# A two-layer encoder trunk whose matmuls walk their columns backwards

## The chip, the cores and the metric

The kernel runs on one NeuronCore of a Trainium2 chip. The metric is the device time of one execution in microseconds (us), lower is better. A profile of one execution was recorded for the kernel before the change; its times are those of the instructions on each engine: TensorE (PE, with its weight loads as PEld), VectorE (DVE), ScalarE (ACT), GpSimd (POOL), and SyncE (SP), which issues the DMAs.

## The reference

Two inputs of 512 tokens by 1024 features, "prompt" and "sample", pass through the same two layers. Layer 0 is differential attention, layer 1 a bidirectional retention; each is preceded by an RMS norm and added to the residual, and a final RMS norm closes the trunk. Cut to what matters:

```python
# layer 0, per token block
proj = h @ w_in                        # 1024 -> 8192: q, k, v, gate
q = rotary_half(q) * DA_HEAD_DIM ** -0.5; k = rotary_half(k)
p = softmax(q @ k.T)                   # two maps per head, 8 heads
a = p[:, :, 0] - lam * p[:, :, 1]
o = rms_norm(a @ v, subln_g) * (1 - lambda_init)
x = x + (o * silu(gate)) @ w_out       # 2048 -> 1024

# layer 1
proj = h @ w_in                        # 1024 -> 6144: q, k, v, gate
scores = (q @ k.T) * decay_mask        # within a chunk; forward and backward in time
o = scores @ v + (q * decay) @ state   # state carries k.T @ v of the other chunks
x = x + (rms_norm(o, subln_g) * silu(gate)) @ w_out

y = rms_norm(x, final_norm_g)
```

## The kernel before

**Precision.** Operands are split in two: `hi`, the value rounded to the type fp32r (a copy on ScalarE, `hi_of`, line 399), and `lo`, the value minus `hi` (a subtraction on VectorE, `lo_of`, line 402). A product is three matmuls, hi by hi, hi by lo and lo by hi, accumulated in one PSUM bank (`PASSES`, line 32). So every product below is a run of matmuls in threes. The transposes (lines 606, 716, 815, 1028, 1040, 1161) and eight warm-up matmuls at the start (line 1010) work on plain fp32.

**Projections.** Both input projections go by one step of Strassen's scheme: seven products P1 to P7 instead of eight, whose inputs are sums and differences of blocks. The combined activations are made once per layer (`make_b`, line 448) and stay on chip as `b` tiles or in the `arena`. Class `Unit` (line 518) handles a strip of weights: `prep` combines and splits a weight block, `product` runs the matmuls, `evac` empties the banks. A "pair" unit holds weights as the stationary operand and moves 512 tokens (line 599); a "wide" unit holds activations and moves 256 weight columns into half a bank (line 609).

**Attention and retention.** `scores` (line 1107) makes a 128 by 512 block of scores per map (line 1116); maximum (`row_max`, line 1124), exponential (line 1134), combination and transpose follow (line 1161), then `av` (line 1170) multiplies by the values in 24 matmuls of 256 columns (line 1181). For the retention, `score2` (line 1315), `state2` (line 1339) and `av2` (lines 1359 and 1367) do the like in chunks of 256 tokens.

**Output projection.** `out_step` (line 871) runs six matmuls of 512 columns into a bank (line 891), and VectorE adds the bank, scaled, to the residual. The very last one is done in two halves of 256 columns.

**Order.** All operations are recorded in a `Plan` (line 69) with an assumed cost and with what they read and write. `Plan.arrange` lists them by those costs and by their due times, and the instructions are then issued in that order on each engine's queue. PSUM has four kinds of banks: `pj` (3), `sc` (2), `o` (2) and `tp` (1). The costs handed to the plan are constants in the code (for instance 2.79 us for a pair product of twelve matmuls, line 620), so the order doesn't depend on how a matmul addresses its columns.

A matmul call names the bank, the stationary operand, the moving operand, and whether it opens and closes the accumulation. The one at line 599:

```python
nc.tensor.matmul(
    ps.t, a[u][0]()[:, k, :], bt[k][:, v, :], start=(opens and k == 0 and i == 0),
    stop=(k == 3 and i == 2), skip_group_check=True)
```

The first argument is the output (a bank `ps`, 128 partitions by 512 fp32 columns), the second the stationary operand (128 by 128), the third the moving operand, 128 by 512.

Of the kernel before, what the change touches and what calls it, by code (L numbers as in the profile page):

```python
# [15 lines left out]
P = 128  # L16
# [237 lines left out]
def trunk_kernel(  # L254
# [7 lines left out]
    nc = tc.nc  # L262
# [255 lines left out]
    class Unit:  # L518
# [67 lines left out]
        def product(self, op):  # L586
            which = BANK_OF[op]
            n_banks = 2 if self.wide else 1
            opens = op in OPENS
            if opens:  # L590
                self.banks[which] = [bank(self.tags[which], which) for _ in range(n_banks)]
            a, b = self.ops.pop(op), B_OF[op]
            bt = [Bop[b, k] for k in range(4)]
            reads = [q[1] for q in a] + bt

            def pair(ps, ks=range(4)):
                for k in ks:
                    for i, (u, v) in enumerate(PASSES):
                        nc.tensor.matmul(  # L599
                            ps.t, a[u][0]()[:, k, :], bt[k][:, v, :], start=(opens and k == 0 and i == 0),  # L600
                            stop=(k == 3 and i == 2), skip_group_check=True)

            def wide(ps, t):
                if self.led and op == "P1" and t == 0:
                    for j in range(NT):
                        nc.tensor.transpose(ps[:, j * P:(j + 1) * P], ident.t, ident.t)
                for k in range(4):
                    for i, (u, v) in enumerate(PASSES):
                        nc.tensor.matmul(  # L609
                            ps[:, (t % 2) * 256:(t % 2) * 256 + 256], bt[k][:, v, t * P:(t + 1) * P],  # L610
                            a[u][0]()[:, k, :], start=(opens and t % 2 == 0 and k == 0 and i == 0),
                            stop=(k == 3 and i == 2), skip_group_check=True)

            if not self.wide:
                ps = self.banks[which][0]
                if op == "P1" and self in first_units[:2]:
                    for k in range(4):
                        pe(0.7, lambda k=k: pair(ps, (k,)), reads[:2] + [bt[k]], [(ps, k)])
                else:
                    pe(2.79, lambda: pair(ps), reads, [ps])  # L620
                return
            for t in range(NT):
                ps = self.banks[which][t // 2]
                led = self.led and op == "P1" and t == 0
                pe(1.87 if led else 1.43, lambda ps=ps, t=t: wide(ps, t), reads + [ident] * led, [ps])
# [245 lines left out]
    def out_step(w, h, g, t, i, o, rr, last, parts=1):  # L871


        owed[h, g] -= 1
        if (h, i) not in wsn:
            out_weights(w, h, i)
        banks = [bank("pj") for _ in range(parts)]
        u = wsn[h, i]
        x = xN[g, t]
        n = S // parts  # L880
        for p in range(parts):
            here = slice(p * n, (p + 1) * n)
            part = (x, i) if parts == 1 else (x, (i, p))

            ps = banks[p]

            def fn(here=here, ps=ps):
                m = 0
                for e in range(2):
                    for a, b in PASSES:  # L890
                        nc.tensor.matmul(ps[:, here], o[a][:, e, t * P:(t + 1) * P], u[b][:, e, here],  # L891
                                         start=(m == 0), stop=(m == 5))
                        m += 1
            pe(1.39 / parts, fn, [(o[0], t // 2), (o[1], t // 2), *u], [ps])
            half = x[:, i * S + p * n:i * S + (p + 1) * n]
            axpy(n, lambda half=half, here=here, ps=ps: nc.vector.scalar_tensor_tensor(  # L896
                half, ps[:, here], rr[:, t % 2:t % 2 + 1], half, op0=ALU.mult, op1=ALU.add),
                [ps, part, rr], [part])
            if h == NH - 1:
                last(g, t, i, half, n, part, i == 1 and p == parts - 1)  # L900
# [206 lines left out]
    def scores(i):  # L1107
        h, g, t = tiles[i]
        st[i]['s'] = []
        for j in range(2):  # L1110
            s = bank("sc")
            q, k = qk[h, g, j, 0], qk[h, g, j, 1]

            def fn(s=s, q=q, k=k):
                for n, (a, b) in enumerate(PASSES):
                    nc.tensor.matmul(s.t, q[:, a, t * P:(t + 1) * P], k[:, b, :], start=(n == 0), stop=(n == 2))  # L1116
            pe(0.7, fn, [q, k], [s])
            st[i]['s'].append(s)

# [50 lines left out]
    def av(i):  # L1170

        h, g, t = tiles[i]
        aT, v = st[i]['aT'], vt[h, g]
        o = bank("o")

        def fn():
            n = 0
            for e in range(2):
                for a, b in PASSES:
                    for j in range(NT):  # L1180
                        nc.tensor.matmul(o[:, e * 256:(e + 1) * 256], v[b][:, j, e * P:(e + 1) * P], aT[a][:, j, :],  # L1181
                                         start=(n == 0), stop=(n % 12 == 11), skip_group_check=True)
                        n += 1
        pe(2.76, fn, [*aT, *v], [o])
        if t == 0:
            settle(h - 1, g)
            oT[h, g] = new_oT(g)
        st[i].update(o=o, sq=weigh(o, sg[h, g], oT[h, g], t // 2, GUARD))
# [117 lines left out]
    def score2(b, c):  # L1306

        h, g = blocks[b]
        s = bank("sc", "s2")
        q, k = qk[b, 0], qk[b, 1]  # L1310

        def fn():
            for j in range(2):
                for i, (u, v) in enumerate(PASSES):
                    nc.tensor.matmul(  # L1315
                        s[:, j * 256:(j + 1) * 256], k[:, u, (2 * c + j) * P:(2 * c + j + 1) * P],
                        q[:, v, c * 256:(c + 1) * 256], start=(j == 0 and i == 0), stop=(i == 2),
                        skip_group_check=True)
        pe(0.71, fn, [q, k], [s])
        t1 = e_t("rt")  # L1320
        F = Fs[h]
        dve(S, lambda: nc.vector.tensor_tensor(
            t1.t, s.t, F[:, 0:4, :].rearrange("p a b -> p (a b)"), op=ALU.mult),
            [s, *((F, n) for n in range(4))], [t1])
        aT = slot(8 + 2 * (b % 2) + c, [P, 2, S], F32R, 16)
        hi_of(S, lambda: aT[:, 0, :], lambda: t1.t, [t1], [(aT, 0)])
        lo_of(S, lambda: aT[:, 1, :], lambda: t1.t, lambda: aT[:, 0, :], [t1, (aT, 0)], [(aT, 1)])
        aTs[b, c] = aT

    def state2(b, c):  # L1330

        s = bank("tp", "state")
        kt, v_ = kts[b], vt[b]

        def fn():
            for j in range(2):
                for i, (u, v) in enumerate(PASSES):
                    t = 2 * c + j
                    nc.tensor.matmul(s[:, 0:256], kt[:, u, t * P:(t + 1) * P], v_[v][:, t, :],  # L1339
                                     start=(j == 0 and i == 0), stop=(j == 1 and i == 2))  # L1340
        pe(0.71, fn, [kt, *v_], [s])
        if b not in Ss:
            Ss[b] = slot(12 + b % 2, [P, 2, 2, 256])
        S_ = Ss[b]
        hi_of(256, lambda: S_[:, 0, c, :], lambda: s[:, 0:256], [s], [(S_, (0, c))])
        lo_of(256, lambda: S_[:, 1, c, :], lambda: s[:, 0:256], lambda: S_[:, 0, c, :], [s, (S_, (0, c))],
              [(S_, (1, c))])

    def av2(b, c):

        h, g = blocks[b]
        o, far = bank("o"), bank("o")
        a_, v_, q, S_, F = aTs[b, c], vt[b], qk[b, 0], Ss[b], Fs[h]

        def near():
            for e in range(2):
                for j in range(2):
                    for i, (u, v) in enumerate(PASSES):
                        nc.tensor.matmul(  # L1359
                            o[:, e * 256:(e + 1) * 256], v_[v][:, 2 * c + j, e * P:(e + 1) * P],  # L1360
                            a_[:, u, j * 256:(j + 1) * 256], start=(e == 0 and j == 0 and i == 0),
                            stop=(j == 1 and i == 2), skip_group_check=True)

        def other():
            for e in range(2):
                for i, (u, v) in enumerate(PASSES):
                    nc.tensor.matmul(  # L1367
                        far[:, e * 256:(e + 1) * 256], S_[:, v, 1 - c, e * P:(e + 1) * P],
                        q[:, u, c * 256:(c + 1) * 256], start=(e == 0 and i == 0), stop=(i == 2),
                        skip_group_check=True)  # L1370
        pe(1.38, near, [a_, *v_], [o])
        pe(0.69, other, [q, (S_, (0, 1 - c)), (S_, (1, 1 - c))], [far])
# [161 lines left out]
```

## Time and profile before

| | before |
|---|---|
| median of 3 runs | 1808.89 us (1808.3 to 1814.46) |
| profiled execution, first to last instruction (span) | 1807.0 us |
| instructions | 27780 |
| TensorE busy | 1794.9 us, 99% |
| VectorE, ScalarE, GpSimd busy | 1477.1 us (82%), 895.1 us (50%), 169.5 us (9%) |
| granted TensorE clock, mean | 0.999 |
| DMA | 328.81 MB, mean 182 GB/s |

The profiled execution's own time is its span; the page gives no other time for it, and the span lies 1.9 us below the median of the runs. "Busy" is the time in which at least one instruction of the engine was running. Matmuls are pipelined: the row of one begins before the row of the one ahead of it has ended, so a group's mean duration is longer than the distance between two matmuls, and the distance is what a run of them costs. The ends of matmul rows are modelled by the profiler, the starts are recorded.

### The profile page before, as it was taken

What the parts mean: (1) busy time and instruction counts of PE and PEld (TensorE: products, weight loads), DVE (VectorE), ACT (ScalarE), POOL (GpSimd) and SP (SyncE); (2) the same over time, 40 slices, a digit from 0 to 9 for tenths busy, and PEclk for the clock granted to TensorE, in tenths of its full rate; (3) what the DMA queues carried; (4) which work ended last, traced back from release to release, by engine and by line L of the source; (5) the groups of instructions that cost most, each with busy time, mean ns of one, the idle gap of its engine ahead of it and who ended that gap; (6) DMA issues with size and microseconds to landing.
All of it is one profiled execution on the core that took longest, in us unless ns stands there. A gap on an engine that the chain in (4) does not pass through costs nothing.

```text
span 1807.0 us, 27780 instructions
## 1 busy us (share of the span) xinstructions
PE 1794.9 (99%) x10299; PEld 1558.1 (86%) x10299; DVE 1477.1 (82%) x2319; ACT 895.1 (50%) x1856; POOL 169.5 (9%) x323
## 2 busy tenths in 40 slices
PE   9999999999999999999999999999999999999998
PEld 6789889898988888888888888898989898888887
DVE  7958787778699888888888897787887967888887
ACT  7753444433434565554555866444434355444346
POOL 1000000000000022222322300000000000111113
PEclk9999999999999999999999999999999999999999
DMA  6444455555545685444554524464657559765662
GB/s 217 134 126 137 161 140 178 184 168 155 174 126 175 201 334 198 178 156 159 190 204 140 190 73 146 140 210 146 205 156 228 151 170 396 272 238 182 225 218 94
DMA packets 162767, 328.81 MB, mean 182 GB/s; under 512 B 12724, under 2 KB 76872, under 8 KB 162632
## 3 DMA queue, kind: packets, MB, share of 16 engines
q1 hardware_dynamic: 162304, 326.71, 54.1%
q8 instruction: 81, 1.33, 0.3%
q14 instruction: 54, 0.44, 0.1%
q10 hardware_dynamic: 328, 0.34, 0.1%
HBM read 209.55 MB, written 117.44 MB: 181 GB/s over the span
## 4 chain that ended last, share of the span: by engine, by line
PE 93%; DVE 2%; DMA 2%; ACT 2%; issue 1%; POOL 0%; SPq 0%; POOLq 0%; DVEq 0%; ACTq 0%
PE pj L599 20%; PE pj L891 19%; PE sc L599 10%; PE pj L609 10%; PE o L599 8%; PE o L1181 5%; PE sc L1116 5%; PE sc L609 5%; PE o L609 2%; PE o L1359 2%; PE tp L1161 2%; PE sc L1315 1%; PE o L1367 1%; PE tp L1339 1%; DMA raw<-in_ret_w_out_dram 1%
## 5 line engine op out<-in xcount | busy, mean ns | idle before, releaser
L891 PE MATMUL pj<-ws,arena 128*128 128x512 f32 x1542 | 391.2, 397 | 0.0
L891 PEld LDWEIGHTS pj<-ws,arena 128*128 128x128 f32 x1542 | 277.7, 188 | 52.7
L599 PE MATMUL pj<-b,ws 128*128 128x512 f32 x1080 | 265.0, 392 | 0.0
L599 PEld LDWEIGHTS pj<-b,ws 128*128 128x128 f32 x1080 | 201.4, 188 | 43.0
L403 DVE TENSOR_TENSOR ws<-st,ws 128x512 fp32r<-128x512 f32 (+1 forms) x192 | 147.9, 774 | 74.8 <-ACT ws L400 56.7
L896 DVE SCALAR_TENSOR_TENSOR b<-pj,crr,b 128x512 f32<-128x512 f32 (+1 forms) x257 | 189.9, 744 | 21.4 <-PE pj L891 21.0
L403 DVE TENSOR_TENSOR ws<-raw,ws 128x512 fp32r<-128x512 f32 (+1 forms) x164 | 141.5, 868 | 71.3 <-ACT ws L400 61.0
L400 ACT CAST ws<-st 128x512 fp32r<-128x512 f32 (+1 forms) x192 | 132.4, 693 | 121.4 <-PE pj L599 36.4
L599 PE MATMUL sc<-arena,ws 128*128 128x512 f32 x768 | 186.8, 392 | 0.0
L599 PE MATMUL o<-arena,ws 128*128 128x512 f32 x744 | 180.0, 393 | 1.1 <-ACT m L385 0.6
L599 PEld LDWEIGHTS sc<-arena,ws 128*128 128x128 f32 x768 | 144.0, 188 | 31.3
L400 ACT CAST ws<-raw 128x512 fp32r<-128x512 f32 (+1 forms) x164 | 125.7, 772 | 87.0 <-PE o L599 45.0
L599 PEld LDWEIGHTS o<-arena,ws 128*128 128x128 f32 x744 | 138.4, 188 | 31.7 <-DVE arena L463 1.4
L599 PE MATMUL pj<-arena,ws 128*128 128x512 f32 x648 | 160.3, 392 | 0.4 <-DVE arena L463 0.4
L599 PEld LDWEIGHTS pj<-arena,ws 128*128 128x128 f32 x648 | 120.8, 188 | 26.7 <-DVE arena L463 0.7
L1134 ACT ACTIVATE b<-sc,nm 128x512 f32<-128x512 f32 x128 | 88.0, 689 | 66.9 <-DVE nm L1124 66.5
L636 ACT COPY c<-pj 128x512 f32<-128x512 f32 x104 | 60.9, 586 | 119.7 <-PE pj L599 66.4
L609 PE MATMUL pj<-ws,b 128*128 128x256 f32 x960 | 116.8, 276 | 0.0
L609 PEld LDWEIGHTS pj<-ws,b 128*128 128x128 f32 x960 | 113.2, 188 | 0.7
L1116 PE MATMUL sc<-arena 128*128 128x512 f32 x384 | 101.2, 395 | 0.3 <-ACT b L1134 0.3
L1181 PEld LDWEIGHTS o<-arena 128*128 128x128 f32 x768 | 93.1, 188 | 2.7
L1181 PE MATMUL o<-arena 128*128 128x256 f32 x768 | 93.7, 278 | 0.0
(207 smaller groups left out, 2855.9 us busy)
## 6 DMA issues: line engine op xcount, KB each, us to landing
qk<-os SPq DMA_DIRECT2D x192, 256.0 KB, 3.6
arena<-qk SPq DMA_DIRECT2D x96, 512.0 KB, 5.8
raw<-in_da_w_in_dram SPq DMA_DIRECT2D x64, 512.0 KB, 5.1
v<-os SPq DMA_DIRECT2D x64, 512.0 KB, 4.3
arena<-v SPq DMA_DIRECT2D x64, 512.0 KB, 4.1
raw<-in_ret_w_in_dram SPq DMA_DIRECT2D x48, 512.0 KB, 4.8
os<-g SPq DMA_DIRECT2D x32, 512.0 KB, 7.4
g<-e SPq DMA_DIRECT2D x48, 256.0 KB, 4.6
```

The source lines that it names most:

```text
L400: act(n, lambda: nc.scalar.copy(dst(), src()), r, w)
L403: dve(n, lambda: nc.vector.tensor_tensor(dst(), src(), hi().bitcast(F32), op=ALU.subtract), r, w)
L599: nc.tensor.matmul(ps.t, a[u][0]()[:, k, :], bt[k][:, v, :], start=(opens and k == 0 and i == 0), stop=(k == 3 and i == 2), skip_group_che ...
L609: nc.tensor.matmul(ps[:, (t % 2) * 256:(t % 2) * 256 + 256], bt[k][:, v, t * P:(t + 1) * P], a[u][0]()[:, k, :], start=(opens and t % 2 == ...
L636: act(S, lambda c=c, ps=ps: nc.scalar.copy(c.t, ps.t), [ps], [c])
L891: nc.tensor.matmul(ps[:, here], o[a][:, e, t * P:(t + 1) * P], u[b][:, e, here], start=(m == 0), stop=(m == 5))
L896: axpy(n, lambda half=half, here=here, ps=ps: nc.vector.scalar_tensor_tensor(half, ps[:, here], rr[:, t % 2:t % 2 + 1], half, op0=ALU.mult ...
L1116: nc.tensor.matmul(s.t, q[:, a, t * P:(t + 1) * P], k[:, b, :], start=(n == 0), stop=(n == 2))
L1134: act(840, lambda j=j, s=s, m=m: nc.scalar.activation(p[:, j, :], s.t, AF.Exp, bias=m.t, accum_out=sm[:, 2 * j + n:2 * j + n + 1]), [s, m] ...
L1161: nc.tensor.transpose(tp[:, j * P:(j + 1) * P], p[:, 0, j * P:(j + 1) * P], ident.t)
L1181: nc.tensor.matmul(o[:, e * 256:(e + 1) * 256], v[b][:, j, e * P:(e + 1) * P], aT[a][:, j, :], start=(n == 0), stop=(n % 12 == 11), skip_g ...
L1359: nc.tensor.matmul(o[:, e * 256:(e + 1) * 256], v_[v][:, 2 * c + j, e * P:(e + 1) * P], a_[:, u, j * 256:(j + 1) * 256], start=(e == 0 and ...
```

## The change

In all matmuls but the transposes and the warm-up, the moving operand is indexed with a step of -1 along its columns, and so is the output. Column 511 is read first and its result goes to column 511 of the bank; column 0 comes last. What stands in the bank afterwards is the same. The stationary operand, the number of matmuls, the plan's costs and all other instructions stay as written.

```diff
--- before.py
+++ after.py
@@ -597,7 +597,7 @@
                 for k in ks:
                     for i, (u, v) in enumerate(PASSES):
                         nc.tensor.matmul(
-                            ps.t, a[u][0]()[:, k, :], bt[k][:, v, :], start=(opens and k == 0 and i == 0),
+                            ps[:, ::-1], a[u][0]()[:, k, :], bt[k][:, v, ::-1], start=(opens and k == 0 and i == 0),
                             stop=(k == 3 and i == 2), skip_group_check=True)
 
             def wide(ps, t):
@@ -607,8 +607,8 @@
                 for k in range(4):
                     for i, (u, v) in enumerate(PASSES):
                         nc.tensor.matmul(
-                            ps[:, (t % 2) * 256:(t % 2) * 256 + 256], bt[k][:, v, t * P:(t + 1) * P],
-                            a[u][0]()[:, k, :], start=(opens and t % 2 == 0 and k == 0 and i == 0),
+                            ps[:, (t % 2) * 256:(t % 2) * 256 + 256][:, ::-1], bt[k][:, v, t * P:(t + 1) * P],
+                            a[u][0]()[:, k, ::-1], start=(opens and t % 2 == 0 and k == 0 and i == 0),
                             stop=(k == 3 and i == 2), skip_group_check=True)
 
             if not self.wide:
@@ -888,7 +888,7 @@
                 m = 0
                 for e in range(2):
                     for a, b in PASSES:
-                        nc.tensor.matmul(ps[:, here], o[a][:, e, t * P:(t + 1) * P], u[b][:, e, here],
+                        nc.tensor.matmul(ps[:, here][:, ::-1], o[a][:, e, t * P:(t + 1) * P], u[b][:, e, here][:, ::-1],
                                          start=(m == 0), stop=(m == 5))
                         m += 1
             pe(1.39 / parts, fn, [(o[0], t // 2), (o[1], t // 2), *u], [ps])
@@ -1113,7 +1113,8 @@
 
             def fn(s=s, q=q, k=k):
                 for n, (a, b) in enumerate(PASSES):
-                    nc.tensor.matmul(s.t, q[:, a, t * P:(t + 1) * P], k[:, b, :], start=(n == 0), stop=(n == 2))
+                    nc.tensor.matmul(s[:, ::-1], q[:, a, t * P:(t + 1) * P], k[:, b, ::-1],
+                                     start=(n == 0), stop=(n == 2))
             pe(0.7, fn, [q, k], [s])
             st[i]['s'].append(s)
 
@@ -1178,7 +1179,8 @@
             for e in range(2):
                 for a, b in PASSES:
                     for j in range(NT):
-                        nc.tensor.matmul(o[:, e * 256:(e + 1) * 256], v[b][:, j, e * P:(e + 1) * P], aT[a][:, j, :],
+                        nc.tensor.matmul(o[:, e * 256:(e + 1) * 256][:, ::-1], v[b][:, j, e * P:(e + 1) * P],
+                                         aT[a][:, j, ::-1],
                                          start=(n == 0), stop=(n % 12 == 11), skip_group_check=True)
                         n += 1
         pe(2.76, fn, [*aT, *v], [o])
@@ -1313,8 +1315,8 @@
             for j in range(2):
                 for i, (u, v) in enumerate(PASSES):
                     nc.tensor.matmul(
-                        s[:, j * 256:(j + 1) * 256], k[:, u, (2 * c + j) * P:(2 * c + j + 1) * P],
-                        q[:, v, c * 256:(c + 1) * 256], start=(j == 0 and i == 0), stop=(i == 2),
+                        s[:, j * 256:(j + 1) * 256][:, ::-1], k[:, u, (2 * c + j) * P:(2 * c + j + 1) * P],
+                        q[:, v, c * 256:(c + 1) * 256][:, ::-1], start=(j == 0 and i == 0), stop=(i == 2),
                         skip_group_check=True)
         pe(0.71, fn, [q, k], [s])
         t1 = e_t("rt")
@@ -1336,7 +1338,7 @@
             for j in range(2):
                 for i, (u, v) in enumerate(PASSES):
                     t = 2 * c + j
-                    nc.tensor.matmul(s[:, 0:256], kt[:, u, t * P:(t + 1) * P], v_[v][:, t, :],
+                    nc.tensor.matmul(s[:, 0:256][:, ::-1], kt[:, u, t * P:(t + 1) * P], v_[v][:, t, ::-1],
                                      start=(j == 0 and i == 0), stop=(j == 1 and i == 2))
         pe(0.71, fn, [kt, *v_], [s])
         if b not in Ss:
@@ -1357,16 +1359,16 @@
                 for j in range(2):
                     for i, (u, v) in enumerate(PASSES):
                         nc.tensor.matmul(
-                            o[:, e * 256:(e + 1) * 256], v_[v][:, 2 * c + j, e * P:(e + 1) * P],
-                            a_[:, u, j * 256:(j + 1) * 256], start=(e == 0 and j == 0 and i == 0),
+                            o[:, e * 256:(e + 1) * 256][:, ::-1], v_[v][:, 2 * c + j, e * P:(e + 1) * P],
+                            a_[:, u, j * 256:(j + 1) * 256][:, ::-1], start=(e == 0 and j == 0 and i == 0),
                             stop=(j == 1 and i == 2), skip_group_check=True)
 
         def other():
             for e in range(2):
                 for i, (u, v) in enumerate(PASSES):
                     nc.tensor.matmul(
-                        far[:, e * 256:(e + 1) * 256], S_[:, v, 1 - c, e * P:(e + 1) * P],
-                        q[:, u, c * 256:(c + 1) * 256], start=(e == 0 and i == 0), stop=(i == 2),
+                        far[:, e * 256:(e + 1) * 256][:, ::-1], S_[:, v, 1 - c, e * P:(e + 1) * P],
+                        q[:, u, c * 256:(c + 1) * 256][:, ::-1], start=(e == 0 and i == 0), stop=(i == 2),
                         skip_group_check=True)
         pe(1.38, near, [a_, *v_], [o])
         pe(0.69, other, [q, (S_, (0, 1 - c)), (S_, (1, 1 - c))], [far])
```

## The prediction

> **What bounds the kernel now.** I read the page first: its busy row, its slices, its chain by engine.
>
> ```profile
> span 1807.0 us, 27780 instructions
> PE 1794.9 (99%) x10299; PEld 1558.1 (86%) x10299; DVE 1477.1 (82%) x2319; ACT 895.1 (50%) x1856; POOL 169.5 (9%) x323
> PE   9999999999999999999999999999999999999998
> PEclk9999999999999999999999999999999999999999
> PE 93%; DVE 2%; DMA 2%; ACT 2%; issue 1%; POOL 0%; SPq 0%; POOLq 0%; DVEq 0%; ACTq 0%
> ```
>
> TensorE is busy in 1794.9 of 1807.0 us, in every one of the 40 slices, at the full granted clock, and it carries 93% of the chain that ended last. A busy matmul row may still hide waiting, so the next view is the list of waits, TensorE's rows alone (engine, line, whom it waited for; us in total, times, longest).
>
> ```profile
> PE sc L1010 <- DVE minus L411: 1.4, 1, 1.4
> PE tp L1028 <- DVE arena L463: 1.0, 2, 0.7
> PE o L1028 <- DVE b L387: 0.6, 1, 0.6
> PE o L599 <- ACT m L385: 0.6, 1, 0.6
> PE pj L599 <- DVE arena L463: 0.4, 1, 0.4
> PE o L599 <- DVE arena L463: 0.3, 2, 0.2
> PE sc L1116 <- ACT b L1134: 0.3, 1, 0.3
> PE tp L815 <- DVE b L403: 0.2, 1, 0.2
> ```
>
> These come to 4.8 us in all. The kernel is one stream of matmuls from end to end, and whatever one matmul gains or loses lands in the span undiluted.
>
> Third, how many matmuls the change touches, and what each costs. The view by windows over the whole span, restricted to one source line at a time, gives the count in brackets; the rows below are lines 599, 609, 891, 1116, 1181, 1315, 1339, 1359 and 1367 in that order. The last row, from the groups with shapes kept apart, is the 256-column part of line 891.
>
> ```profile
> core 0: us, PE busy (x), PEclk, DMA share, GB/s
> 0.00:1807.00 1807.00, 780.90 (x3360) 1.00 0.55 182
> 0.00:1807.00 1807.00, 310.33 (x2688) 1.00 0.55 182
> 0.00:1807.00 1807.00, 391.16 (x1542) 1.00 0.55 182
> 0.00:1807.00 1807.00, 101.24 (x384) 1.00 0.55 182
> 0.00:1807.00 1807.00, 93.68 (x768) 1.00 0.55 182
> 0.00:1807.00 1807.00, 27.96 (x192) 1.00 0.55 182
> 0.00:1807.00 1807.00, 27.57 (x192) 1.00 0.55 182
> 0.00:1807.00 1807.00, 48.93 (x384) 1.00 0.55 182
> 0.00:1807.00 1807.00, 27.05 (x192) 1.00 0.55 182
> L891 PE MATMUL pj<-ws,arena 128*128 128x256 f32 x12 | 1.6, 280 | 0.0
> ```
>
> The counts add to 9702 of the 10299 matmuls. Lines 599 and 1116 and all but 12 of line 891 have 512 columns: 3360 + 384 + 1530 = 5274. The other 4428 have 256. Busy times of groups overlap at their edges, since a matmul's row is longer than the distance to the next one, so the price of one is taken from the chain of waits, whose pieces follow each other without overlap (start us, us, what, count).
>
> ```profile
> 289.66 5.47 PE pj L609 x48
> 303.34 5.44 PE sc L609 x48
> 344.30 8.24 PE pj L599 x36
> 1783.58 13.76 PE pj L891 x60
> ```
>
> A 512-column matmul takes 8.24 / 36 = 228.9 ns of the stream (line 891: 13.76 / 60 = 229.3), a 256-column one 5.47 / 48 = 114.0 ns. That is twice the time for twice the columns, so nearly all of it is paid per column: 0.447 ns each. The changed matmuls hold 5274 x 0.2289 + 4428 x 0.1140 = 1207.2 + 504.8 = 1712 us, 95% of the span. Hence the scale for everything below: **1 ns more per changed matmul is 9.7 us, 0.54% of the time**; one per cent on the column is 17 us.
>
> **The change, part by part.** It adds and removes no matmul, no DMA and no evacuation. A listing of the two programs engine by engine shows every queue in the same order (10407 instructions on TensorE in both), TensorE waiting on the same semaphores, and 9702 matmuls whose moving operand and output have step -1 from the last element in place of +1 from the first. Weight loads are untouched, and so are the transposes and the warm-up at line 1010. Sum for queues, transfers and moved steps: 0 us.
>
> One by-product: 19 row maxima at line 1124 also wait for ScalarE, and 5 subtractions at line 403 no longer wait for TensorE, a net 14 more wait instructions on VectorE.
>
> ```profile
> L1124 DVEq EVENT_SEMAPHORE  x52: 21/21/21, 660.4 to 1002.7; - x52
> ```
>
> At 21 ns each that is 14 x 0.021 = 0.3 us, on an engine that is idle 18% of the span. What the added wait names, an exponential two tiles back, is done by then, because the score matmul that fills the bank waits for the exponential of the tile before. Queued behind it is VectorE's next work, and behind that the exponentials, which already wait for this line; TensorE waited 0.3 us for them in the whole run. Cost 0, and without that cover 19 x 0.021 = 0.4 us.
>
> What is left is the one question: does a column that is read and written backwards cost what a forward one costs? The trace of before has no matmul of either kind with a backward step, so it is bounded from both sides by the nearest rows.
>
> From below: the quickest run of 48 among those above took 5.44 us against 5.47, 0.55% less. If every changed matmul were that quick, 0.0055 x 1712 = 9.4 us would go. These matmuls hardly vary, so a backward order that dodged other engines' accesses would find little to dodge.
>
> From above: two rows show TensorE passing columns more slowly, both full fp32 rather than fp32r, both of steps that the change leaves alone. The first is from the timeline, four transposes in a row; the others are group rows with the mean ns of one.
>
> ```profile
> 657.25 0.60 PE L1161 MATMUL tp<-ident,b 128*128 128x128 f32 x4
> L1161 PE MATMUL tp<-ident,b 128*128 128x128 f32 x256 | 38.4, 272 | 0.0
> L1010 PE MATMUL sc<-e 128*128 128x512 f32 x16 | 10.1, 800 | 1.4 <-DVE minus L411 1.4
> ```
>
> The transposes stand (600 - 272) / 3 = 109 ns apart for 128 columns, 0.854 ns a column: half the rate of the changed matmuls. The warm-up stands (10.1 - 0.8) / 15 = 0.62 us apart for 512 columns.
>
> In between is a small price paid per matmul. Two equal runs of line 1181 from the timeline show how far such a price varies today:
>
> ```profile
> 643.21 2.89 PE L1181 MATMUL o<-arena 128*128 128x256 f32 x24
> 653.72 2.99 PE L1181 MATMUL o<-arena 128*128 128x256 f32 x24
> ```
>
> 0.10 us over 23 distances is 4.3 ns a matmul.
>
> I take zero. The rows nearest in kind are the matmuls themselves: same type, same operands, same bytes, and within any aligned group of neighbouring elements the backward walk touches the same elements, only in the other order. 512 and 256 columns are whole multiples of any such group. The slow rows come from another data type. Sum: 1807.0 + 0 = 1807.0 us of span; the median of the runs stands 1.9 us above the profiled span, so 1809.
>
> [...]
>
> **The rivals.** *Half rate.* The reader of the moving operand, or the writer of the bank, takes neighbouring elements together only when the addresses rise; backwards each column is an access of its own, and the stream runs at the transposes' 0.854 ns. A 512-column matmul then takes 437 ns (+208.3), a 256-column one 219 (+104.6): 5274 x 0.2083 + 4428 x 0.1046 = 1099 + 463 = 1562 us, and the time is 3371. For it: the changed rate is so close to twice that of the transposes that some pairing may lie behind it. Against it: pairs need no direction. It decides from 0.93 ns per matmul, 0.4% of a long one; there is no cover, as TensorE is the bound everywhere.
>
> *A small price per matmul.* A backward stream starts or ends a little less tightly against the next. With the 4.3 ns above, 9702 x 4.3 = 42 us: 1851. For it: 1 ns is enough. Against it: length and price are now proportional, which leaves little fixed price to disturb.
>
> *Much worse.* The fast pass of fp32r is lost altogether and the warm-up's 0.62 us per 512 columns applies: 5274 x 0.391 + 4428 x 0.196 = 2930 us more, 4739. For it: only that the transposes and the warm-up, the plain fp32 work, run slower at all. Against it: the type of the operand is unchanged.
>
> *Faster.* The bound from below everywhere: 1809 - 9.4 = 1799.5.
>
> That the change does not do what it says, because reading and writing backwards together are turned forward again before the chip, would look like no change; the listing, with step -1 in all 9702, speaks against it.
>
> **How the numbers follow.** No change 0.40; half rate 0.30; small price 0.15; much worse 0.10; faster 0.05. No change is the likeliest single case and gives the forecast, 1809; its own range is 0.5% either way, 1800 to 1818, and 0.5% is about what a measurement of this kernel can tell from none (the three runs span 0.34%). Because the slow cases hold more than half together, the range has to reach the half rate: 1800 to 3400, which leaves out much worse and faster, 0.15. Faster by over 0.5%: 0.05; within: 0.40; slower: 0.30 + 0.15 + 0.10 = 0.55.
>
> **What would show it.** In the chain of waits after, 48 of line 609 stay at 5.4 to 5.5 us and 36 of line 599 at 8.2 to 8.3 if I am right. Under half rate they read 10.5 and 15.7, and VectorE's and ScalarE's shares fall by nearly half with unchanged busy times. A small price shows as equal nanoseconds on both lengths, a price per column as twice as many on the long ones. Waits of TensorE stay near 5 us in every case; if they rise by tens of us, or the order of a queue differs, my reasoning was wrong at its root, not in its size.

## Result and the profile after

The changed kernel takes 1848.8 us (median; 1848.45 to 1849.6), the kernel before 1808.7 in the same session: ratio 1.0215, 95% interval 1.0201 to 1.0230. It is 40 us slower. The forecast was no change at 1809; the time lies nearest the rival with a small price for each matmul, 1851.

The page of the changed kernel, busy row, slices and chain:

```profile
span 1846.8 us, 27794 instructions
PE 1835.6 (99%) x10299; PEld 1578.8 (85%) x10299; DVE 1480.8 (80%) x2319; ACT 895.6 (48%) x1856; POOL 169.6 (9%) x323
PE   9999999999999999999999999999999999999998
PEclk9999999999999999999999999999999999999999
PE 93%; DVE 2%; DMA 2%; ACT 1%; issue 1%; POOL 0%; SPq 0%; POOLq 0%; DVEq 0%; ACTq 0%
```

The span grew by 39.8 us and TensorE's busy time by 40.7, at the same granted clock (0.999) and with the same share of the chain (93%). VectorE and ScalarE did the same work in the same time, within 4 us. TensorE's list of waits sums to 3.8 us against 4.8. So TensorE waits no longer: the matmuls themselves take longer. The chain of waits says how much (start us, us, what, count):

```profile
272.84 8.40 PE pj L599 x36
295.24 5.76 PE pj L609 x48
309.46 5.65 PE sc L609 x48
1823.07 14.02 PE pj L891 x60
```

A 512-column matmul of line 599 went from 228.9 to 8.40 / 36 = 233.3 ns (+4.4), those at the end of line 891 from 229.3 to 233.7 (+4.4). A 256-column one of line 609 went from 113.3 to 114.0 up to 117.7 to 120.0, about +4 to +7. The short matmul pays at least as much as the long one, so this is no price per column: that would be twice as much on the long ones. The windows view shows where it adds up, lines in the order of the prediction (1181 to 1367 now stand at 1182, 1317, 1341, 1361 and 1369):

```profile
0.00:1847.00 1847.00, 795.49 (x3360) 1.00 0.53 178
0.00:1847.00 1847.00, 325.18 (x2688) 1.00 0.53 178
0.00:1847.00 1847.00, 395.78 (x1542) 1.00 0.53 178
0.00:1847.00 1847.00, 102.66 (x384) 1.00 0.53 178
0.00:1847.00 1847.00, 95.81 (x768) 1.00 0.53 178
0.00:1847.00 1847.00, 28.04 (x192) 1.00 0.53 178
0.00:1847.00 1847.00, 28.06 (x192) 1.00 0.53 178
0.00:1847.00 1847.00, 50.97 (x384) 1.00 0.53 178
0.00:1847.00 1847.00, 28.16 (x192) 1.00 0.53 178
```

Against before these are +14.6, +14.9, +4.6, +1.4, +2.1, +0.1, +0.5, +2.0 and +1.1 us: 41.3 in all. It isn't uniform. Line 1317, already at 27.96 us for 192 before, pays next to nothing (0.4 ns a matmul); lines 609, 1361 and 1369 pay the most, 5.3 to 5.8 ns. Whatever causes it depends on more than the direction.

### The profile page after: what moved, and what is told of

Read it like the earlier page. It is cut to its first block, busy times and chain, and to the rows that moved or that the text cites. A ratio compares the mean times of both kernels' runs of the same rounds, so it can differ in the third digit from the quotient of the medians.

```text
span 1846.8 us, 27794 instructions
## 1 busy us (share of the span) xinstructions
PE 1835.6 (99%) x10299; PEld 1578.8 (85%) x10299; DVE 1480.8 (80%) x2319; ACT 895.6 (48%) x1856; POOL 169.6 (9%) x323
## 4 chain that ended last, share of the span: by engine, by line
PE 93%; DVE 2%; DMA 2%; ACT 1%; issue 1%; POOL 0%; SPq 0%; POOLq 0%; DVEq 0%; ACTq 0%
PE pj L599 20%; PE pj L891 19%; PE sc L599 10%; PE pj L609 10%; PE o L599 8%; PE sc L609 5%; PE o L1182 5%; PE sc L1116 5%; PE o L609 2%; PE o L1361 2%; PE tp L1162 1%; PE o L1369 1%; PE tp L1341 1%; PE sc L1317 1%; DMA raw<-in_ret_w_out_dram 1%
## 5 line engine op out<-in xcount | busy, mean ns | idle before, releaser
L891 PE MATMUL pj<-ws,arena 128*128 128x512 f32 x1542 | 395.8, 401 | 0.0
L599 PE MATMUL pj<-b,ws 128*128 128x512 f32 x1080 | 269.7, 397 | 0.0
L609 PE MATMUL pj<-ws,b 128*128 128x256 f32 x960 | 122.0, 282 | 0.0
L609 PEld LDWEIGHTS pj<-ws,b 128*128 128x128 f32 x960 | 118.1, 188 | 0.8
```

The lines of the kernel that those rows point to most:

```text
L599: nc.tensor.matmul(ps[:, ::-1], a[u][0]()[:, k, :], bt[k][:, v, ::-1], start=(opens and k == 0 and i == 0), stop=(k == 3 and i == 2), skip ...
L609: nc.tensor.matmul(ps[:, (t % 2) * 256:(t % 2) * 256 + 256][:, ::-1], bt[k][:, v, t * P:(t + 1) * P], a[u][0]()[:, k, ::-1], start=(opens ...
L891: nc.tensor.matmul(ps[:, here][:, ::-1], o[a][:, e, t * P:(t + 1) * P], u[b][:, e, here][:, ::-1], start=(m == 0), stop=(m == 5))
```

## The experiments

Kernels that read but do not write backwards, or read shifted or reordered columns, work on columns out of place; they do the same number of matmuls of the same sizes. Ratios are against the kernel before, run beside them.

### Read or write?

```diff
-ps[:, ::-1], a[u][0]()[:, k, :], bt[k][:, v, ::-1],
+ps.t, a[u][0]()[:, k, :], bt[k][:, v, ::-1],        # e1, and alike in all nine calls
+ps[:, ::-1], a[u][0]()[:, k, :], bt[k][:, v, :],    # e2
```

> All 9702 matmuls read their moving operand backwards but write the bank forwards, so the columns of each bank are mirrored and the outputs are not the reference's; the work is the same. If the price sits in the backward read: 1849 us, 36 of line 599 at 8.40 us, 48 of line 609 at 5.76, as with both. If it sits in the backward write: 1809, 8.24 and 5.47. If each bears a part: in between, 1820 to 1840.

> All 9702 matmuls read forwards and write the bank backwards; again mirrored banks, same work. The mirror of the run that only reads backwards: 1849 us if the price sits in the write, 1809 if it sits in the read, in between if shared. If both this and the other come out at 1849, the price is paid once for a backward step on either side.

Reading backwards alone: 1849.3 us, ratio 1.0217 (1.0200 to 1.0234). Writing backwards alone: 1808.6 us, 0.9996 (0.9984 to 1.0007). Chain rows of the read-only run first; the chain of the write-only run stands where it stood before:

```profile
216.11 8.40 PE pj L599 x36
173.41 5.76 PE sc L609 x48
```

```profile
209.72 8.24 PE pj L599 x36
168.76 5.44 PE sc L609 x48
```

That settles the side: the whole price is in the read of the moving operand, and writing a bank from its last column down costs nothing here (8.24 and 5.44 us in the chain, as before).

### Long or short matmuls?

Both directions backwards, but only in some of the nine calls: lines 599, 891 and 1116 (e3), or the other six (e4); the rest as before.

> Both directions backwards at lines 599, 891 and 1116 alone (the 5274 matmuls of 512 columns; the 12 halves of 256 in line 891 too); the other 4416 forwards. If a column costs more: 70% of the columns are here, so +28 us of the +40, 1837. If the price is the same for each matmul: 54% of the matmuls, +22, 1831. From the spacing in the chain after (8.40 / 36 against 8.24 / 36, 4.4 ns) times 5274: +23, 1832.

> Both directions backwards in the 4416 matmuls of 256 columns at lines 609, 1181, 1315, 1339, 1359 and 1367 alone. Per column: +12 us, 1821. Same price for each matmul: +18, 1827. From the spacing in the chain after (5.76 / 48 against 5.47 / 48, 6.0 ns) times 4416: +27, 1835. With the run of 512 columns alone the two gains should add up to 40.

1829.1 us, ratio 1.0105 (1.0089 to 1.0122), and 1828.3 us, 1.0104 (1.0086 to 1.0121). The two increases, 20.0 and 19.2 us, add to 39.2 of the 40. A price per column would have split them 28 to 12, and that is ruled out; one price for every matmul, 22 to 18, comes closest. The figures I multiplied up from the chain were too high for the short matmuls (19 against 27): by busy time line 609 rose by 4.9 ns a matmul in this run, since its rows stand at 5.65 us in the first part and at 5.76 only later, and the other five lines by 3.3. Two chain rows of line 609 in e4:

```profile
168.92 5.65 PE sc L609 x48
1291.47 5.76 PE sc L609 x48
```

### What about a backward read costs?

Four reads that share one feature each with the backward one. The bank is written forwards in all of them.

```diff
+h = t.rearrange("p (h n) -> p h n", h=2); return h[:, ::-1, :]   # e5: upper half first, each half forwards
+return t[:, ::-1] if i == 1 else t                                # e6: one pass of three backwards
+h = t.rearrange("p (n h) -> p h n", h=2); return h                # e7: even columns, then odd ones
+at = a * t.shape[2] + lo + (-1 if a == last else 1)               # e8: forwards, one element off
```

> All 9702 matmuls read the upper half of their columns first and then the lower half, each half forwards (step +1 inside, -256 or -128 outside); the bank is written forwards, so halves come out exchanged. If the price belongs to the negative innermost step: 1809 us, 36 of line 599 at 8.24. If it belongs to a stream that begins above where it ends (the first address is not the lowest): 1849, 8.40, and 48 of line 609 at 5.76. If each turn back inside a matmul has its own price: between or above.

> Only the second of each three passes reads backwards (3234 of the 9702 matmuls), so one bank in three passes is mirrored. If each backward matmul pays for itself: a third of +40, 1822 us, 12 of line 599 at (8 x 228.9 + 4 x 233.3) = 2.76. If the price is for a change of direction or for a jump between the end of one stream and the start of the next: two of three boundaries change, +27, 1836 or more.

> All 9702 matmuls read forwards with step +2, first the even columns and then the odd ones; the bank is written in order, so columns are shuffled. If only a step below zero costs: 1809 us. If any innermost step other than +1 costs the same fixed price: 1849. If a step of 2 halves what one fetch yields and fetching is the bound: far above, up to the 3371 of the half-rate case.

> Forward reads as in the kernel before, but in lines 599, 609 and 891 (7590 of the 9702 matmuls) the moving operand starts one element after or before its place, so its first address is no longer a multiple of 64 bytes; values come from the neighbouring column, the work is the same. If the backward price is that of a first address inside a group of columns (a backward stream starts at the last one): as in the changed kernel for these lines, about +33 us, 1842. If it is the step: 1809.

*Halves exchanged:* 1809.0 us, ratio 1.0000 (0.9988 to 1.0013). A stream that begins above where it ends costs nothing, so the first address being the higher one isn't it.

*One element off, all forwards:* 1842.9 us, ratio 1.0181 (1.0165 to 1.0197). This was the surprise: with no backward step anywhere, the 7590 shifted matmuls pay what backward ones pay (the prices of these three lines in the changed kernel add to 34.1 us). So it takes no negative step to pay this price. Chain rows:

```profile
213.67 8.38 PE pj L605 x36
170.87 5.76 PE sc L615 x48
```

*One pass of three:* 1839.0 us, ratio 1.0160 (1.0144 to 1.0176). A third of the matmuls backward costs three quarters of the price, not the third expected of matmuls that pay for themselves. The chain shows where:

```profile
212.61 8.28 PE pj L604 x36
170.01 5.76 PE sc L614 x48
```

In most of the chain's rows the long ones (line 599, here 604) pay a quarter, 8.24 to 8.28 where all backward gave 8.40; a few rows stand at 8.40. The short ones (line 609, here 614) pay in full: 16 backward matmuls put the mean of all 48 at 120 ns. So what a matmul pays is not settled by its own direction alone; its neighbours take part in it.

*Step of two:* 3491 us, ratio 1.9289 (1.9259 to 1.9320). Group rows of this run, then chain rows:

```profile
L609 PE MATMUL pj<-b,ws 128*128 128x512 f32 x1080 | 510.2, 649 | 0.0
L619 PEld LDWEIGHTS pj<-ws,b 128*128 128x128 f32 x960 | 200.0, 208 | 24.4 <-issue 3.9
```

```profile
390.31 16.32 PE pj L609 x36
307.94 11.04 PE sc L619 x48
```

16.32 / 36 = 453 ns and 11.04 / 48 = 230 ns, twice the forward figures. So the half rate that I kept as a rival exists, per column and on the read side, but a step of -1 doesn't set it off. The weight loads, which this kernel does not touch, take 208 ns here against 188: a first sign that the two streams of TensorE, matmuls and weight loads, bear on each other.

### Is it the alignment of the first address?

That was my next theory, since 512 backward columns start at the last of 16 elements that begin at a multiple of 64 bytes from the start of their tile. The e8 edit again, with other shifts; in the third kernel the shifted read is turned backwards, so that it starts at a multiple of 16 elements.

```diff
-at = a * t.shape[2] + lo + (-1 if a == last else 1)
+at = a * t.shape[2] + lo + (-16 if a == last else 16)    # e9
+at = a * t.shape[2] + lo + (-4 if a == last else 4)      # e10
+at = a * t.shape[2] + lo + (-15 if a == last else 1)     # e11, and [:, ::-1] behind it
```

> The run shifted by one, with a shift of 16 elements (64 bytes) instead: forward reads in lines 599, 609 and 891, 7590 matmuls, values from 16 columns further on. If the price there came from the first address not being a multiple of some number of bytes up to 64: 1809 us, 48 of line 609 at 5.47. If it came from reading across the border of the hi and lo halves, or from the extra overlap itself: 1842, as with a shift of one.

> The same with a shift of 4 elements (16 bytes). If only 16 bytes matter: 1809. If the group is larger, 32 or 64 bytes: 1842.

> Lines 599, 609 and 891 (7590 matmuls) read backwards, but from one element higher, or 15 lower where one higher lies outside the tile, so that the first address is a multiple of 16 elements; the other matmuls read forwards, and all banks are written forwards. If the backward price is only that of a first address inside a group: 1809. If a backward step costs by itself: the same share as the changed kernel for these lines, about +33, 1842. If what counts is how many aligned groups of 16 a stream touches (17 or 33 here against 16 or 32 in the changed kernel): 1842 or above.

Shift 16: 1828.4 us, ratio 1.0108 (1.0093 to 1.0123). Shift 4: 1834.3, 1.0139 (1.0124 to 1.0155). Backward from a multiple of 16: 1855.9, 1.0259 (1.0242 to 1.0276), dearer with 7590 matmuls than the changed kernel with 9702. The theory falls: a stream that starts at a multiple of 64 bytes from the start of its tile, as all did before, still pays, and starting a backward stream at such a place does not save it. Nor does one price fit all. Chain rows of the three, in the order of the text:

```profile
211.40 8.24 PE pj L605 x36
169.01 5.73 PE sc L615 x48
1802.79 13.93 PE pj L897 x60
```

```profile
214.48 8.32 PE pj L605 x36
172.11 5.71 PE sc L615 x48
```

```profile
215.48 8.48 PE pj L605 x36
172.54 5.76 PE sc L615 x48
```

With shift 16 the long matmuls of line 599 stay at 8.24, free, while the short ones of line 609 go to 5.73. The two lines differ in length and in where their weights lie. Length alone doesn't tell payers from the rest: line 891 (here 897), as long as line 599, went from 13.76 to 13.93 us for 60. The group rows point to the weights: the weight loads, not shifted, went from 188 to 190 ns. First two rows of the kernel before, then the same two with the shift of 16 (line 609 is 615).

```profile
L609 PE MATMUL pj<-ws,b 128*128 128x256 f32 x960 | 116.8, 276 | 0.0
L609 PEld LDWEIGHTS pj<-ws,b 128*128 128x128 f32 x960 | 113.2, 188 | 0.7
```

```profile
L615 PE MATMUL pj<-ws,b 128*128 128x256 f32 x960 | 122.3, 282 | 0.0
L615 PEld LDWEIGHTS pj<-ws,b 128*128 128x128 f32 x960 | 118.4, 190 | 0.7
```

### Where the two streams stand to each other

Each matmul has a weight load of 128 columns, and the trace shows the loads running beside the matmuls (PEld busy 86%, PE 99%). If what counts is the place of the moving operand against that of the weights, then shifting both must undo what shifting one does, and shifting the weights alone must cost though the moving operand is untouched.

```diff
+    at = a * t.shape[2] + lo
+    at += 16 if at + 16 + n <= t.shape[1] * t.shape[2] else -48
...
+V(bt[k].t, v, t * P, P), V(a[u][0](), k, 0, 256),     # line 609: weights and moving operand
+V(v_[v].t, 2 * c + j, e * P, P),                      # line 1359: weights alone
```

> All reads forward; two separate stages are edited. At line 609 (2688 matmuls, the projections) weights and moving operand both start 16 elements further on, or 48 earlier at a tile's end; with the moving operand alone shifted, 48 of them had taken longer, about 5.75 us. At line 1359 (384 matmuls, the retention) only the weights are shifted. If what counts is where the two streams, weight load and moving operand, stand to each other: line 609 is back at 5.44 to 5.47 for 48, and line 1359 rises from 113 to about 118 ns apart though its moving operand is untouched; 384 x 5 ns = 2 us, 1811 in all. If what counts is the moving operand's own first address: line 609 stays near 5.75 (+16 us) and line 1359 at 113 ns, 1825.

1810.2 us, ratio 1.0020 (1.0001 to 1.0039). Chain rows first, then the groups (line 609 is 616, line 1359 is 1368):

```profile
209.75 8.24 PE pj L606 x36
168.81 5.44 PE sc L616 x48
```

```profile
L616 PE MATMUL pj<-ws,b 128*128 128x256 f32 x960 | 116.7, 276 | 0.0
L1368 PE MATMUL o<-arena 128*128 128x256 f32 x384 | 50.9, 282 | 0.0
L1368 PEld LDWEIGHTS o<-arena 128*128 128x128 f32 x384 | 49.9, 190 | 2.3
```

With both shifted, line 609 is back at 5.44 for 48 and 276 ns a matmul, where the shift of the moving operand alone gave 5.73 and 282. Two things besides the weights differ between the two runs. At a tile's end the operand starts 48 elements back here and 16 back there; but there the other three quarters of the line's matmuls, with the same shift as here, stand 118 to 120 ns apart as well. And lines 599 and 891 are not shifted here; the 48 matmuls of a row, though, follow each other with no other line between them.

Line 1359, with its weights shifted and its moving operand where it was, went from 48.9 us and 276 ns to 50.9 and 282. That half is weaker, since the same line (1361 in e3) rose to 50.3 us and 279 ns there without an edit of its own; why it has this second pace is open. For the weights speaks what happened beside it: line 1367, issued in turn with line 1359, rose with it in e3 and stayed at 27.0 us here, and the weight loads of line 1359 take 190 ns here against 188 in e3 and before. Group rows of lines 1359 and 1367 before, in e3 and here:

```profile
L1359 PE MATMUL o<-arena 128*128 128x256 f32 x384 | 48.9, 276 | 0.0
L1367 PE MATMUL o<-arena,b 128*128 128x256 f32 x192 | 27.0, 276 | 0.0
```

```profile
L1361 PE MATMUL o<-arena 128*128 128x256 f32 x384 | 50.3, 279 | 0.0
L1369 PE MATMUL o<-arena,b 128*128 128x256 f32 x192 | 27.8, 279 | 0.0
```

```profile
L1376 PE MATMUL o<-arena,b 128*128 128x256 f32 x192 | 27.0, 276 | 0.0
```

So this is shown for forward streams, at line 609 and a shift of 16: the pace of a matmul depends on where its moving operand stands to its weights (5.44 us for 48 with both shifted, 5.73 with one), and not on the moving operand's address alone. That the backward stream pays for the same reason, because it walks through the relation instead of keeping it, is argued from the like size (8.38 and 5.76 with a shift of one, 8.40 and 5.76 backwards) and not shown; the weight loads of line 609 stay at 188 ns in the changed kernel, as with a shift of one, where the shift of 16 put them at 190. Weights read backwards beside a backward moving operand were not tried, nor was a backward operand with its weights elsewhere. No run beat the kernel before.

## Why the prediction was right or wrong

- *TensorE is the bound and every nanosecond lands in the span:* right. The busy time rose by 40.7 us, the span by 39.8, the waits not at all.
- *Order, transfers and the 14 added wait instructions cost nothing:* right. The write-only kernel, which reads forwards and has the 14 wait instructions too (27794 instructions), stands at 0.9996.
- *"I take zero":* wrong, and it is the step on which the point forecast failed. The reason given, that the backward walk touches the same elements of each aligned group, looked at the moving operand alone, and that columns are read in such groups no run shows. The read-only run puts the whole price in that read, 4.1 ns a matmul, and the shifted reads show that the moving operand isn't alone: its pace depends on where the weights beside it lie (48 of line 609 take 5.73 us with the moving operand shifted by 16, 5.44 with the weights shifted too). That this is also how the backward read comes to pay is argued, not shown. The prediction named weight loads as untouched and left them there.
- *The small price:* the right case, held at 0.15, and its size was close: 4.3 ns a matmul, read off two runs of one line, against a measured 39.8 / 9702 = 4.1. That it came so close is in part luck, since the lines pay from 0.4 to 5.8 ns, and no run shows its reason, a stream that starts or ends less tightly. The argument against it, that price and length are proportional and leave little fixed price to disturb, was the mistake. A short and a long matmul have a weight load of the same size in common (128 columns, 188 ns at line 609 as at line 891); that the price sits there is my estimate, not shown by a run. The sign given to tell it by, like nanoseconds on both lengths rather than twice as many on the long ones, is what the chain shows (4.4 against 4 to 7).
- *Half rate:* not for a step of -1, on either side. Its price was sized well, 3371 against 3491 with a step of 2. That neighbouring columns are taken together, the reason given for it, no run shows.
- *Much worse:* did not happen, and its price was misread. The 0.62 us is the mean of two paces and counts rows, not matmuls: the weight loads of line 1010 start 0.85 us apart at first, its last rows 0.43 us apart, and eight matmuls leave sixteen rows. A plain fp32 matmul of 512 columns thus took 0.86 us once settled, and by that the rival's time would have been about 6500, an estimate.
- *Chances:* slower by over 0.5% had 0.55 and came about; the single likeliest case did not. The range of 1800 to 3400 holds the time, but it was stretched that far for the half rate, which did not happen; the range of the forecast itself, 1800 to 1818, misses it.

## What to carry to other kernels

On a kernel that is one stream of matmuls, the distance between two matmuls in the chain of waits is the number to watch: 4 ns on it was 40 us here, while TensorE's waits (4.8 us before, 3.8 after) and its clock (0.999 in both) stayed about as they were. When an edit changes the addresses of one operand of a matmul, look at the other operand too, and compare matmuls of two lengths, because a price per matmul and a price per column separate at once. Here a backward write into a bank was free (ratio 0.9996), a read in steps of two took 3491 us in place of 1809, and a shift of 16 elements in the moving operand cost up to 6 ns per 256-column matmul of line 609 (5.73 us for 48 against 5.44) until the weights were shifted with it.

## What was unexpected of the hardware

The moving operand and the weight load are not independent: a shift of 64 bytes in the moving operand put 256-column matmuls at 119 to 120 ns in place of 113, the same shift in both put them back at 113. The effect is some 5%, but it is there.

A step of two in the moving operand ran at 453 ns for 512 columns against 229, and at 230 ns for 256 columns against 114. In these matmuls, passing over every other column was not free.
